# A SwiGLU FFN on one core in two parts of 6 and 5 column groups instead of three parts of 3, 4 and 4, with the residual h kept in DRAM in between

## The chip, the core and the metric

The kernel runs on one core of a Trainium2 chip. The metric is the device time of one execution in microseconds (us). The engines are TensorE (PE in the profile, with its weight loads as PEld), VectorE (DVE), ScalarE (ACT), GpSimd (POOL) and SyncE (SP). SP's instruction queue issues the weight loads and the DMA transposes, POOL's queue issues a few other DMAs. Engines and queues each work through their instructions in order and wait for one another by semaphores.

## The reference

Two pre-norm residual layers on a stream h of 256 tokens by 2048 columns, in float32. Layer 0 mixes with windowed attention and an mLSTM, layer 1 with forgetting attention. Each layer ends in the FFN that this study is about, and the last layer is followed by a norm:

```python
def swiglu(xn, w_gate, w_up, w_down):
    return (jax.nn.silu(xn @ w_gate) * (xn @ w_up)) @ w_down

h = h + mix
h = h + swiglu(rms_norm(h, norm_ffn[layer]), w_gate[layer], w_up[layer], w_down[layer])
```

w_gate and w_up are 2048 x 5632, w_down is 5632 x 2048.

## The kernel before

**Precision.** A float32 operand is split in two reduced parts, hi and lo (hi is a cast on ScalarE, lo the difference on VectorE: split_chunk, lines 184 to 191, for weights, split_plain, lines 355 to 357, for the rest). A product is three matmuls: hi x hi, hi x lo, lo x hi (three, lines 531 to 534). x is held as xh and xl, the FFN's middle result as mh and ml, each 16 blocks k of 128 rows by 256 tokens.

**Column groups.** pair_group (lines 539 to 635) computes two products of 512 columns at once (gate and up of the same columns, or two neighbouring column blocks of down), over the blocks k in pairs (256 rows of the weight). The constant ORDER, or DOWN for the down products, says in which order the pairs come and of which kind each is:

- A plain pair, (0, pair): 2 blocks x 2 token halves x 2 products x 3 = 24 matmuls of 512 columns. It loads 2 weight tiles of 512 KB and needs 2 pairs of hi/lo buffers.
- A mixed pair, (1, pair): the seven-product form of a 2 x 2 block product, 7 x 3 = 21 matmuls. It loads the same two tiles, and VectorE forms sums of weight blocks (lines 607 to 610), so that it needs 4 pairs of hi/lo buffers and sums of the left operand as well, made ahead by sums_of (lines 263 to 280) and kept in sx for x and sd for the middle result.

The products of the mixed pairs go to four PSUM banks (prod), the plain ones to four others (plain); from one group to the next the two sets of banks swap (par). Behind its last mixed pair a group combines prod into the tile c (combine, lines 553 to 565: a copy on ScalarE and three additions on VectorE). c has one buffer.

**Weight buffers.** In the FFN there are 8 pairs of hi/lo buffers in a ring (stock, lines 104 to 110 and 773) and 4 raw tiles for loads under way.

**The FFN** (lines 637 to 762). 5632 columns are 11 groups of 512, each a pair_group of gate and up with 8 pairs of which ORDER makes 3 mixed. After it VectorE adds the plain sums to c (line 665), ScalarE applies silu (line 667), VectorE multiplies (line 669). The result has tokens on the partitions and must be transposed to be the down product's left operand: as two 16-bit planes (copies at line 697), by DMA transposes on SP's queue (line 699), and then joined and split into mh and ml within the next group (join, lines 700 to 719, due at step MID or MID_DOWN, steps being positions of the order).

mh and ml hold 16 blocks, so 4 groups. PARTS = (0, 3, 7, 11) therefore makes three parts of 3, 4 and 4 groups; after each part two pair_groups (n0 = 0 and 2) multiply what is there by the matching rows of w_down, and VectorE adds the result to h: c at line 758, the plain sums in add_out (line 370). DOWN makes 2 of 6 pairs mixed in the first part and 3 of 8 in the others. In the first part, whose mh isn't full, the last group takes another way (lines 677 to 692): 8 transposes on TensorE (tile pf), split straight from PSUM. In the last part of layer 1 the second half of the columns is a plain gemm without mixed pairs (lines 743 to 748), and finish (lines 1292 to 1325) applies the final norm.

**Order of the instructions.** The program is written in the order above, and a scheduler places each engine's instructions ahead of time; run_due (lines 198 to 201) puts the due jobs behind a given cast. On the chip each engine keeps that order.

Of the kernel before, what the change touches and what calls it, by code (L numbers as in the profile page):

```python
# [17 lines left out]
P = 128  # L18
# [17 lines left out]
ORDER = ((0, 0), (1, 1), (0, 2), (1, 3), (0, 4), (1, 5), (0, 6), (0, 7))  # L36
HEAVY = ((1, 1), (0, 0), (1, 3), (0, 2), (1, 5), (0, 4), (1, 7), (0, 6))
FOURTH = 7
DENSE = ()
DOWN = {  # L40
    6: ((0, 0), (1, 1), (0, 2), (1, 3), (0, 4), (0, 5)),
    8: ((0, 0), (1, 1), (0, 2), (1, 3), (0, 4), (1, 5), (0, 6), (0, 7)),
}
MID = 6
MID_DOWN = 5
AHEAD = (5, 6)
# [29 lines left out]
def trunk(  # L76
# [278 lines left out]
    def split_plain(dst_h, dst_l, src):  # L355
        nc.scalar.copy(dst_h, src)  # L356
        nc.vector.tensor_tensor(out=dst_l, in0=src, in1=dst_h.bitcast(F32), op=ALU.subtract)  # L357
# [178 lines left out]
    def bank(par, name):  # L536
        return pm.tile([P, NB], F32, tag="pm", name=name) if par else pa.tile([P, NB], F32, tag="acc", name=name)
# [99 lines left out]
    def ffn(layer, fp, sx, x4, sd, key, todo, idx_next=None, key_next=None, finish=None):  # L637
        r = rstd(key)

        def sums_x(pair):  # L640
            if pair == FOURTH:
                return [[m[:, k, P:S] for k in (2, 6, 10)] + [x4[:, a, :]] for a, m in enumerate((xh, xl))]
            j = mixed_of(ORDER).index(pair)
            return four(sx[0], j), four(sx[1], j)

        for g0, g1 in zip(PARTS, PARTS[1:]):
            end = g1 == PARTS[-1]
            nk = 4 * (g1 - g0)
            order = DOWN[nk // 2]
            for g in range(g0, g1):  # L650
                par = (g1 - 1 - g) % 2
# [25 lines left out]
                if g == g1 - 1 and nk < 16:  # L677
                    for half in range(2):
                        pt = bank(par, "pf").rearrange("p (i q) -> p i q", i=2)
                        for i in range(2):  # L680
                            cs = (2 * half + i) * P
                            for t in range(NT):
                                nc.tensor.transpose(pt[:, i, t * P : (t + 1) * P], c[:, t, cs : cs + P], ident)
                        pair = 2 * (g - g0) + half
                        k = 2 * pair
                        split_plain(mh[:, k : k + 2, :], ml[:, k : k + 2, :], pt)
                        if pair in mixed_of(order):
                            j = mixed_of(order).index(pair)
                            sums_of(
                                fp, sd[0][:, j, :, :], sd[1][:, j, :, :], lambda full, pt=pt: nc.scalar.copy(full, pt)  # L690
                            )
                    continue
                cu = c.bitcast(U16).rearrange("p a (n b) -> p a n b", b=2)
                flat = c[:, 2:4, :].bitcast(U16).rearrange("p a n -> p (a n)").rearrange("p (b t n) -> p b t n", b=2, t=NT)
                turned = [fp.tile([P, 4, NT, P], U16, tag="tmp", name="turned") for _ in range(2)]
                for b in range(2):
                    nc.scalar.copy(flat[:, b, :, :], cu[:, 0:2, :, b])
                    for t in range(NT):
                        nc.sync.dma_start_transpose(turned[b][:, :, t, :], flat[:, b, t, :])
                def join(c=c, turned=turned, g=g, g0=g0, order=order):  # L700
# [4 lines left out]
                    k = 4 * (g - g0)  # L705
                    split_plain(
                        mh[:, k : k + 4, :].rearrange("p k s -> p (k s)"), ml[:, k : k + 4, :].rearrange("p k s -> p (k s)"), ct
                    )
                    for half in range(2):
                        pair = 2 * (g - g0) + half  # L710
                        if pair in mixed_of(order):
                            j = mixed_of(order).index(pair)
                            sums_of(
                                fp,
                                sd[0][:, j, :, :],
                                sd[1][:, j, :, :],
                                None,
                                ct[:, half * 512 : (half + 1) * 512].rearrange("p (i t q) -> p i t q", i=2, t=NT),
                            )

                todo = [(MID if g < g1 - 1 else MID_DOWN, join)]

            def sums_d(pair, order=order):
                j = mixed_of(order).index(pair)
                return four(sd[0], j), four(sd[1], j)

            def close(acc, n):
                if not end:
                    add_out(acc, n)
                elif idx_next is None:  # L730
                    finish(acc, n, gf)
                else:
                    add_out(acc, n)
                    if n < 1:
                        todo.append((LATER_DOWN[n], split_turned(idx_next, n, *scrap(fp, n))))
                    else:
                        split_scaled(idx_next, n)
                    square_sum(key_next, n)

            gf = None  # L740
            wd = w_down[layer][4 * g0 * P : 4 * g1 * P, :]
            for n0 in (0, 2):
                if end and idx_next is None and n0 == 2:
                    for n in (2, 3):
                        acc = new_acc()
                        gemm(acc, m_of, wd, n * NB, NB, 0, nk, nk, skew=3 if n == 3 else 1, halved=n == 3)
                        close(acc, n)
                    continue
                plain, c = pair_group(
                    fp, 1 - n0 // 2, m_of, sums_d, [(wd, n0 * NB), (wd, (n0 + 1) * NB)], order, todo  # L750
                )
                todo = []
                if end and idx_next is None:
                    gf = fp.tile([P, D], F32, tag="c", name="gf", bufs=1)
                    nc.gpsimd.dma_start(gf, norm_final.partition_broadcast(P))
                for t in range(NT):
                    o = h[:, t, n0 * NB : (n0 + 2) * NB]
                    nc.vector.tensor_tensor(
                        out=o, in0=c[:, 2 * t : 2 * t + 2, :].rearrange("p a n -> p (a n)"), in1=o, op=ALU.add
                    )  # L760
                for m in range(2):
                    close(plain[m], n0 + m)

    def close_layer(layer, w_out, idx, key, **rest):
        with tc.tile_pool(name=f"fp{layer}", bufs=2) as fp:
            nx = len(mixed_of(ORDER))
            nd = max(len(mixed_of(o)) for o in DOWN.values())
            sx = [fp.tile([P, nx, 4, P], F32R, name=f"sx{i}", bufs=1) for i in range(2)]
# [608 lines left out]
```

## Time and profile before

| | us |
|---|---|
| median of 3 runs | 2077.02 (2076.69 to 2077.94) |
| the profiled execution | 2077.56 |
| its span in the profile | 2075.9 |
| FFN of layer 0, first to last matmul | 322.4 to 1009.4 |
| FFN of layer 1, first to last matmul | 1379.6 to 2067.5 |

A table by stage gives each engine's busy time and, behind an x, its count of instructions in a stretch of the span, then the granted TensorE clock, the busy share of the 16 DMA engines, and GB/s. A row of a group of instructions has the line, the engine, the operation, output <- input, count, busy time and mean ns of one. A row of waits reads "who <- for whom: us in total, times, longest".

### The profile page before, as it was taken

How to read it: one execution, taken by the hardware profiler on the slowest of the kernel's cores; microseconds unless marked ns; L12 is line 12 of the kernel's file. 1: busy time of each engine (PE TensorE's matmuls, PEld its weight loads, DVE VectorE, ACT ScalarE, POOL GpSimd, SP SyncE). 2: the span in 40 equal slices, each digit the busy share in tenths (PEclk: the TensorE clock that was granted, in tenths of full speed). 3: DMA queues.
4: the chain of work that ended last, by engine and by line, in shares of the span. 5: the costliest groups of instructions: out<-in, count | busy, mean ns of one | idle time of the engine just before them, and what ended most of it. 6: DMA issues, size and time to landing. Idle time of an engine off the chain costs nothing.

```text
span 2075.9 us, 26965 instructions
## 1 busy us (share of the span) xinstructions
PE 2065.7 (100%) x9473; PEld 1715.1 (83%) x9473; DVE 1819.0 (88%) x2367; ACT 1373.7 (66%) x1744; POOL 44.6 (2%) x66
## 2 busy tenths in 40 slices
PE   9999999999999999999999999999999999999998
PEld 7878888888888888888888888888888888888886
DVE  6788769999999999999899688689999999999994
ACT  6777678664676656667676776687655666556763
POOL 1010000000000000000000001000000000000000
PEclk9999999999999999999999999999999999999999
DMA  8566577666677666766676776586756677667764
GB/s 292 169 216 192 188 244 238 206 219 196 210 223 224 193 208 217 222 204 183 206 213 209 231 201 183 155 268 217 233 187 218 209 217 224 202 195 225 206 196 141
DMA packets 309576, 434.88 MB, mean 209 GB/s; under 512 B 106412, under 2 KB 114624, under 8 KB 309312
## 3 DMA queue, kind: packets, MB, share of 16 engines
q1 hardware_dynamic: 307088, 426.27, 66.1%
q0 software_dynamic: 1632, 5.80, 0.8%
q8 instruction: 74, 1.21, 0.2%
q10 hardware_dynamic: 720, 1.09, 0.2%
q14 instruction: 62, 0.51, 0.1%
HBM read 408.68 MB, written 2.12 MB: 198 GB/s over the span
## 4 chain that ended last, share of the span: by engine, by line
PE 97%; DVE 1%; ACT 1%; issue 1%; DMA 0%; POOLq 0%; POOL 0%; ACTq 0%; DVEq 0%
PE acc L532 21%; PE acc L534 21%; PE acc L533 21%; PE acc L223 6%; PE acc L222 6%; PE acc L224 6%; PE prod L532 5%; PE prod L533 5%; PE prod L534 5%; PE p L386 1%; PE po L487 1%; ACT s L420 0%; PE po L488 0%; DVE lo L188 0%; DMA raw<-in_w_down_dram 0%
## 5 line engine op out<-in xcount | busy, mean ns | idle before, releaser
L188 DVE TENSOR_TENSOR lo<-raw,hi 128x1024 fp32r<-128x1024 f32 (+3 forms) x656 | 771.1, 1195 | 135.5 <-ACT hi L187 133.0
L187 ACT CAST hi<-raw 128x1024 fp32r<-128x1024 f32 (+3 forms) x656 | 661.7, 1027 | 341.2 <-PE acc L534 137.2
L533 PE MATMUL acc<-lo,xh 128*128 128x512 f32 x1320 | 514.0, 389 | 0.0
L534 PE MATMUL acc<-hi,xl 128*128 128x512 f32 x1320 | 511.4, 389 | 0.0
L532 PE MATMUL acc<-hi,xh 128*128 128x512 f32 x1320 | 506.2, 390 | 0.0
L534 PEld LDWEIGHTS acc<-hi,xl 128*128 128x128 f32 x1320 | 247.8, 188 | 51.6
L533 PEld LDWEIGHTS acc<-lo,xh 128*128 128x128 f32 x1320 | 247.8, 188 | 51.4 <-issue 0.2
L532 PEld LDWEIGHTS acc<-hi,xh 128*128 128x128 f32 x1320 | 247.7, 188 | 51.3 <-issue 0.2
L356 ACT CAST hi<-raw 128x512 fp32r<-128x512 f32 x204 | 166.9, 819 | 160.7 <-PE acc L534 83.6
L357 DVE TENSOR_TENSOR lo<-raw,hi 128x512 fp32r<-128x512 f32 x204 | 191.6, 939 | 11.4 <-ACT hi L356 10.4
L533 PE MATMUL acc<-lo,mh 128*128 128x512 f32 x466 | 181.0, 389 | 0.0
L534 PE MATMUL acc<-hi,ml 128*128 128x512 f32 x466 | 180.3, 389 | 0.0
L532 PE MATMUL acc<-hi,mh 128*128 128x512 f32 x466 | 176.2, 389 | 0.1
L356 ACT CAST hi<-t 128x1024 fp32r<-128x1024 f32 x95 | 100.0, 1053 | 63.9 <-PE acc L534 38.0
L357 DVE TENSOR_TENSOR lo<-t,hi 128x1024 fp32r<-128x1024 f32 x95 | 116.2, 1224 | 15.2 <-ACT hi L356 15.0
L223 PE MATMUL acc<-lo,mh 128*128 128x512 f32 (+1 forms) x322 | 126.3, 392 | 0.0
L222 PE MATMUL acc<-hi,mh 128*128 128x512 f32 (+1 forms) x322 | 125.8, 391 | 0.0
L224 PE MATMUL acc<-hi,ml 128*128 128x512 f32 (+1 forms) x322 | 123.7, 391 | 0.0
L532 PEld LDWEIGHTS acc<-hi,mh 128*128 128x128 f32 x466 | 87.5, 188 | 18.5 <-ACT hi L187 0.5
L534 PEld LDWEIGHTS acc<-hi,ml 128*128 128x128 f32 x466 | 87.5, 188 | 18.2
L533 PEld LDWEIGHTS acc<-lo,mh 128*128 128x128 f32 x466 | 87.4, 188 | 18.2
L223 PE MATMUL acc<-lo,xh 128*128 128x512 f32 (+3 forms) x288 | 100.0, 348 | 0.2 <-DVE lo L188 0.2
(356 smaller groups left out, 3174.7 us busy)
## 6 DMA issues: line engine op xcount, KB each, us to landing
raw<-in_w_gate_dram SPq DMA_DIRECT2D x176, 512.0 KB, 4.5
raw<-in_w_up_dram SPq DMA_DIRECT2D x176, 512.0 KB, 4.6
raw<-in_w_down_dram SPq DMA_DIRECT2D x176, 512.0 KB, 4.8
raw<-in_w_in_odd_dram SPq DMA_DIRECT2D x88, 512.0 KB, 5.3
raw<-in_w_in_even_dram SPq DMA_DIRECT2D x51, 512.0 KB, 5.1
raw<-in_w_out_even_dram SPq DMA_DIRECT2D x32, 512.0 KB, 5.2
raw<-in_w_out_odd_dram SPq DMA_DIRECT2D x32, 512.0 KB, 4.7
hr<-in_w_in_even_dram SPq DMA_DIRECT2D x12, 512.0 KB, 4.5
```

Of the source, the lines that this page charges most:

```text
L187: latest[0] = nc.scalar.copy(hi[:, k, 0:n], raw[:, k, 0:n])
L188: nc.vector.tensor_tensor(out=lo[:, k, 0:n], in0=raw[:, k, 0:n], in1=hi[:, k, 0:n].bitcast(F32), op=ALU.subtract)
L222: nc.tensor.matmul(o, ah[:, ts], hi, start=(k == 0), stop=False)
L223: nc.tensor.matmul(o, ah[:, ts], lo, start=False, stop=False)
L224: nc.tensor.matmul(o, al[:, ts], hi, start=False, stop=(k == k_all - 1 and cs.stop == n))
L356: nc.scalar.copy(dst_h, src)
L357: nc.vector.tensor_tensor(out=dst_l, in0=src, in1=dst_h.bitcast(F32), op=ALU.subtract)
L386: nc.tensor.matmul(pq[j % 2][:, j // 2, :], q_of(j, b), k_of(j)[:, 0:cols], start=True, stop=True)
L487: nc.tensor.matmul(po, v_of(j, 0), tt[:, j, 0:2, :].rearrange("p c q -> p (c q)"), start=True, stop=False)
L532: nc.tensor.matmul(o, ah, hi, start=start, stop=False)
L533: nc.tensor.matmul(o, ah, lo, start=False, stop=False)
L534: nc.tensor.matmul(o, al, hi, start=False, stop=stop)
```

## The change

PARTS becomes (0, 6, 11): 6 groups, a down product of 12 pairs, 5 groups, a down product of 10 pairs. Room for the extra blocks of the middle result comes from h. At the start of the FFN h is stored to DRAM (kept) on POOL's queue, in two halves, and the buffer of h takes the blocks from 16 on (the tile more). The first part's down result isn't added to h by VectorE: VectorE adds the plain sums to c, and an accumulating DMA on POOL's queue adds c to kept. At the start of the second part h is loaded back. In the second part the blocks from 16 on (over) are in the buffers of sx, which are free by then. 4 pairs of each down product are mixed: 1, 3, 5, 7 of 12 and 1, 3, 5, 8 of 10; the sums of the fourth have no room in sd and lie in an unused part of mh and ml, or in over. All groups now take the way of the DMA transposes; the branch with transposes on TensorE is gone. Line numbers of the changed kernel differ.

```diff
+NK2 = 8
 DOWN = {
-    6: ((0, 0), (1, 1), (0, 2), (1, 3), (0, 4), (0, 5)),
-    8: ((0, 0), (1, 1), (0, 2), (1, 3), (0, 4), (1, 5), (0, 6), (0, 7)),
+    12: tuple((int(pair in (1, 3, 5, 7)), pair) for pair in range(12)),
+    10: tuple((int(pair in (1, 3, 5, 8)), pair) for pair in range(10)),
 }
+DOWN_FOURTH = {12: 7, 10: 8}
-PARTS = (0, 3, 7, 11)
+PARTS = (0, 6, 11)
...
+        kept = dp.tile([P, NT, D], F32, name=f"kept{layer}")
+        for cs in (slice(0, D // 2), slice(D // 2, D)):
+            nc.gpsimd.dma_start(kept[:, :, cs], h[:, :, cs])
...
         for g0, g1 in zip(PARTS, PARTS[1:]):
...
+            if end:
+                h = cp.tile([P, NT, D], F32, tag="h", name="h")
+                for cs in (slice(0, D // 2), slice(D // 2, D)):
+                    nc.gpsimd.dma_start(h[:, :, cs], kept[:, :, cs])
+            else:
+                more = cp.tile([P, 2, NK2, S], F32R, tag="h", name="more")
+                over = more[:, 0, :, :], more[:, 1, :, :]
+            def room_of(pair, order=order, fourth=fourth, end=end):
+                if pair != fourth:
+                    j = mixed_of(order).index(pair)
+                    return sd[0][:, j, :, :], sd[1][:, j, :, :]
+                if end:
+                    return tuple(m[:, 4:6, :].rearrange("p a (b q) -> p (a b) q", b=2) for m in over)
+                return mh[:, 2:15:4, P:S], ml[:, 2:15:4, P:S]
...
-                if g == g1 - 1 and nk < 16:
-                    for half in range(2):
-                        pt = bank(par, "pf").rearrange("p (i q) -> p i q", i=2)
-                        for i in range(2):
-                            cs = (2 * half + i) * P
-                            for t in range(NT):
-                                nc.tensor.transpose(pt[:, i, t * P : (t + 1) * P], c[:, t, cs : cs + P], ident)
...
-                    continue
...
+            if end:
+                over = [fp.tile([P, 6, S], F32R, tag=f"sx{i}", name=f"over{i}", bufs=1) for i in range(2)]
...
+                if not end:
+                    for m in range(2):
+                        for t in range(NT):
+                            o = c[:, 2 * t + m, :]
+                            nc.vector.tensor_tensor(out=o, in0=plain[m][t], in1=o, op=ALU.add)
+                    nc.gpsimd.dma_start(
+                        kept[:, :, n0 * NB : (n0 + 2) * NB],
+                        c.rearrange("p (t m) n -> p t (m n)", t=NT),
+                        accum_op=ALU.add,
+                    )
+                    continue
```

More of the change, by code (lines that the diff above doesn't have):

```diff
@@ L644, in sums_x, with mid, mid_of @@
             return four(sx[0], j), four(sx[1], j)
+        nonlocal h
+        par = 1
+        kept = dp.tile([P, NT, D], F32, name=f"kept{layer}")
+        for cs in (slice(0, D // 2), slice(D // 2, D)):
+            nc.gpsimd.dma_start(kept[:, :, cs], h[:, :, cs])
+        over = None
+        def mid(k, n):
+            if k < KT:
+                return mh[:, k : k + n, :], ml[:, k : k + n, :]
+            return tuple(m[:, k - KT : k - KT + n, :] for m in over)
+        def mid_of(k):
+            return tuple(m[:, 0, :] for m in mid(k, 1))
         for g0, g1 in zip(PARTS, PARTS[1:]):
@@ L649, in ffn @@
             order = DOWN[nk // 2]
+            fourth = DOWN_FOURTH[nk // 2]
+            if end:
[12 more added lines that the diff above has]
+                return mh[:, 2:15:4, P:S], ml[:, 2:15:4, P:S]
             for g in range(g0, g1):
-                par = (g1 - 1 - g) % 2
+                par = 1 - par
                 plain, c = pair_group(
@@ L676, in ffn @@
                     )
-                if g == g1 - 1 and nk < 16:
-                    for half in range(2):
-                        pt = bank(par, "pf").rearrange("p (i q) -> p i q", i=2)
-                        for i in range(2):
-                            cs = (2 * half + i) * P
-                            for t in range(NT):
[L683 to L691, printed above, removed]
-                    continue
                 cu = c.bitcast(U16).rearrange("p a (n b) -> p a n b", b=2)
@@ L699, in ffn, with join @@
                         nc.sync.dma_start_transpose(turned[b][:, :, t, :], flat[:, b, t, :])
-                def join(c=c, turned=turned, g=g, g0=g0, order=order):
+                def join(c=c, turned=turned, k=4 * (g - g0), order=order, room_of=room_of):
                     ct = c[:, 0:2, :].rearrange("p a n -> p (a n)")
@@ L704, in join @@
                         nc.scalar.copy(cb[:, :, b], turned[b].rearrange("p k t q -> p (k t q)"))
[L705 to L708, printed above, removed]
+                    split_plain(*(m.rearrange("p k s -> p (k s)") for m in mid(k, 4)), ct)
                     for half in range(2):
-                        pair = 2 * (g - g0) + half
+                        pair = k // 2 + half
                         if pair in mixed_of(order):
-                            j = mixed_of(order).index(pair)
                             sums_of(
                                 fp,
-                                sd[0][:, j, :, :],
-                                sd[1][:, j, :, :],
+                                *room_of(pair),
                                 None,
@@ L721, in ffn, with sums_d @@
                 todo = [(MID if g < g1 - 1 else MID_DOWN, join)]
-            def sums_d(pair, order=order):
-                j = mixed_of(order).index(pair)
-                return four(sd[0], j), four(sd[1], j)
+            if end:
+                over = [fp.tile([P, 6, S], F32R, tag=f"sx{i}", name=f"over{i}", bufs=1) for i in range(2)]
+            def sums_d(pair, room_of=room_of):
+                return [[m[:, e, :] for e in range(4)] for m in room_of(pair)]
             def close(acc, n):
-                if not end:
-                    add_out(acc, n)
-                elif idx_next is None:
+                if idx_next is None:
                     finish(acc, n, gf)
-                else:
[L733 to L738, printed above, removed]
+                    return
+                add_out(acc, n)
+                if n < 1:
+                    todo.append((LATER_DOWN[n], split_turned(idx_next, n, *scrap(fp, n))))
+                else:
+                    split_scaled(idx_next, n)
+                square_sum(key_next, n)
             gf = None
@@ L745, in ffn @@
                         acc = new_acc()
-                        gemm(acc, m_of, wd, n * NB, NB, 0, nk, nk, skew=3 if n == 3 else 1, halved=n == 3)
+                        gemm(acc, mid_of, wd, n * NB, NB, 0, nk, nk, skew=3 if n == 3 else 1, halved=n == 3)
                         close(acc, n)
                     continue
+                par = 1 - par
                 plain, c = pair_group(
-                    fp, 1 - n0 // 2, m_of, sums_d, [(wd, n0 * NB), (wd, (n0 + 1) * NB)], order, todo
+                    fp, par, mid_of, sums_d, [(wd, n0 * NB), (wd, (n0 + 1) * NB)], order, todo
                 )
                 todo = []
-                if end and idx_next is None:
+                if not end:
[9 more added lines that the diff above has]
+                    continue
+                if idx_next is None:
                     gf = fp.tile([P, D], F32, tag="c", name="gf", bufs=1)
@@ L766, in close_layer @@
             nx = len(mixed_of(ORDER))
-            nd = max(len(mixed_of(o)) for o in DOWN.values())
-            sx = [fp.tile([P, nx, 4, P], F32R, name=f"sx{i}", bufs=1) for i in range(2)]
+            nd = 3
+            sx = [fp.tile([P, nx, 4, P], F32R, tag=f"sx{i}", name=f"sx{i}", bufs=1) for i in range(2)]
             x4 = fp.tile([P, 2, P], F32R, name="x4", bufs=1)
```

## The prediction

> **What bounds the kernel now.** I read the page first: the busy shares and the chain of work that ended last.
>
> ```profile
> span 2075.9 us, 26965 instructions
> ...
> PE 2065.7 (100%) x9473; PEld 1715.1 (83%) x9473; DVE 1819.0 (88%) x2367; ACT 1373.7 (66%) x1744; POOL 44.6 (2%) x66
> ...
> PE 97%; DVE 1%; ACT 1%; issue 1%; DMA 0%; POOLq 0%; POOL 0%; ACTq 0%; DVEq 0%
> ```
>
> TensorE is idle for 2075.9 - 2065.7 = 10.2 us of the whole span, and the chain runs through it for 97%. VectorE at 88% is a possible second bound. A busy TensorE can still be a slow one, so the next view is the table by stage: five stretches of the FFN, cut where one kind of matmul ends and the next begins, and the last gemm.
>
> ```profile
> core 0: us, PE busy (x) PEld busy (x) DVE busy (x) ACT busy (x) POOL busy (x), PEclk, DMA share, GB/s
> 446.84:510.96 64.12, 64.01 (x286) 52.69 (x285) 60.91 (x71) 34.44 (x39) 0.00 (x0) 1.00 0.63 199
> 676.65:759.61 82.96, 82.96 (x367) 68.69 (x366) 75.82 (x86) 48.31 (x51) 0.00 (x0) 1.00 0.66 209
> 759.61:925.53 165.92, 165.92 (x733) 137.39 (x732) 157.58 (x193) 107.45 (x117) 0.00 (x0) 1.00 0.69 213
> ...
> 1504.05:1567.76 63.71, 63.71 (x286) 52.77 (x285) 60.91 (x71) 34.21 (x39) 0.00 (x0) 1.00 0.63 200
> ...
> 1982.33:2023.81 41.48, 41.48 (x184) 34.35 (x183) 37.55 (x41) 28.92 (x31) 0.00 (x0) 1.00 0.57 179
> 2023.81:2067.51 43.70, 43.70 (x199) 36.29 (x197) 22.81 (x32) 15.47 (x25) 1.15 (x2) 1.00 0.36 122
> ```
>
> The third row is four gate/up groups. By the code each has 3 mixed pairs of 21 matmuls and 5 plain pairs of 24, so 183, and 4 x 183 = 732 (the row counts one more, across the edge). 165.92 / 732 = **0.2267 us** per matmul of 512 columns. The down product of a four-group part (second row) is 2 x 183 = 366 in 82.96 us: 0.2267 again. So while VectorE is 91 to 95% busy (75.82 / 82.96, 157.58 / 165.92), TensorE never waits: the FFN is paced by the number of matmuls. Only the down product of the first, three-group part (first and fourth rows) is longer than its count: 2 x (2 x 21 + 4 x 24) = 276 matmuls are 62.57 us, and the rows have 64.12 and 63.71. The excess is **1.55 us** in layer 0 and **1.14 us** in layer 1. Its contents are the TensorE transposes and, in layer 0, one wait:
>
> ```profile
> L683 PE MATMUL pf<-ident,c x16: 270/272/273, 460.7 to 1520.9; 128*128 128x128 f32 x16
> ```
> ```profile
> 462.57 5.61 DMA raw<-in_w_down_dram
> ...
> 469.16 1.05 ACT hi L187
> 470.21 0.04 issue
> 470.26 0.50 PE acc L532
> ```
>
> The chain of waits there comes from a weight load through ScalarE's cast to a matmul at 470.26. It's the only place inside an FFN where the chain leaves TensorE for long: 1.55 - 1.14 = 0.41 us.
>
> **The change part by part.**
>
> *Matmuls.* Mixed pairs of the down products, each saving 3 matmuls: before, layer 0 has 2 x (2 + 3 + 3) = 16, layer 1 has 2 x 2 + 2 x 3 + 3 = 13 (its last half is a plain gemm). After, layer 0 has 2 x (4 + 4) = 16, layer 1 2 x 4 + 4 = 12. One is lost: 3 x 0.2267 = **+0.68 us**. All other matmuls stay.
>
> *Transposes.* The branch with the 16 TensorE transposes goes; with it go the excess of both rows and the wait at 470: -1.55 - 1.14 = **-2.69 us**. The wait could come back elsewhere (a rival below). In their place the last group of part one is turned by DMA, as all others are: two ScalarE copies out, four DMA transposes on SP's queue, two copies back, a split. SP's queue waits for the copies with weight loads behind it, 20 times already:
>
> ```profile
> SPq L699 <- ACT c L697: 45.2, 20, 4.4
> ACT hi L187 <- PE acc L534: 137.4, 94, 4.6
> ACT hi L356 <- PE acc L534: 121.9, 93, 3.0
> ```
>
> ```profile
> turned<-c SPq DMA_TRANSPOSE x80, 2.5
> ```
>
> SP's wait (45.2 us in 20) is 2.3 us each time, and the stretches that hold those groups run at 0.2267 us per matmul, so two more cost nothing. The cover is in the two ScalarE rows: it waits 94 + 93 = 187 times for TensorE to give a weight buffer back, so it is normally as far ahead as the 8 buffers allow. A mixed pair takes 4, a plain one 2; with the pair in use subtracted that is about one plain pair, 24 x 0.2267 = 5.4 us, ahead (an estimate). Without that cover each would cost up to its 2.3 us. The rows that feed the last pairs must be joined at step 5; they're wanted at pair 8 (second part) or 10 (first), against pair 6 before: later, so free.
>
> *VectorE.* A down pair group now costs it a combine and six additions into h:
>
> ```profile
> L370 DVE TENSOR_TENSOR h<-acc,h 128x512 f32<-128x512 f32 x56 | 36.3, 691 | 3.5 <-PE acc L224 3.5
> L758 DVE TENSOR_TENSOR h<-c,h 128x1024 f32<-128x1024 f32 x22 | 26.0, 1225 | 0.0
> L559 DVE TENSOR_TENSOR c<-prod,c 128x1024 f32<-128x1024 f32 x33 | 40.4, 1223 | 0.0
> L558 DVE TENSOR_TENSOR c<-prod,c 128x512 f32<-128x512 f32 x33 | 22.7, 688 | 0.0
> ```
>
> Combine 2 x 0.69 + 1.22 = 2.60, adding c 2 x 1.23 = 2.45, adding the plain sums 4 x 0.69 = 2.76: 7.81 us. Per layer two whole groups go (15.6) and two more lose the 2.45: -20.5 us, 41 in all, some 2% of 1819. On the path it is worth nothing, since no FFN row shows TensorE waiting for VectorE; a negative bound of zero follows from the 0.2267 in rows where VectorE is 95% busy.
>
> *DMAs.* Per layer POOL's queue stores h (2 x 1 MB), adds two 1 MB tiles to it in DRAM, and loads it back (2 x 1 MB). The trace has no accumulating DMA and no store of this size. The nearest rows are a 1 MB load on POOL's queue, weight loads beside it, and the 11 us from 221 to 232 in which POOL's queue loads 2.1 MB of x:
>
> ```profile
> raw<-in_w_down_dram SPq DMA_DIRECT2D x3, 512.0 KB, 7.2
> gf<-in_norm_final_dram POOLq DMA_DIRECT2D x1, 1024.0 KB, 8.1
> ```
> ```profile
> q0 software_dynamic: 576, 2.10, 49.4%
> q1 hardware_dynamic: 917, 1.77, 46.3%
> ```
> ```profile
> 221.00:232.00 11.00, 11.00 (x59) 9.37 (x58) 8.26 (x13) 5.87 (x7) 2.90 (x4) 1.00 0.96 351
> ```
>
> Both bursts cost TensorE no idle time: 11.00 of 11.00 us here, 43.70 of 43.70 us in the last gemm beside the 8.1 us load. I cost the plain transfers at 0. An accumulate reads two and writes one: bounds 8.1 us (as the load) and 3 x 8.1 x 2 = 48.6 us (three passes, at half the DMA engines as above). I take 2 x 8.1 = 16.2, nearest to the load's row. The Trainium skill, "DMA: Bandwidth & Descriptors", section "Anatomy of one DMA", fits 2.0 us + bytes / 436e3 for a plain DMA of this kind. By it, an estimate, 1 MB takes 4.4 us where the row has 8.1, and three passes 9.2; the sum would be the same.
>
> *The new waits.* (a) c has one buffer, so the next combine's ScalarE copy waits for the accumulate to finish reading; the casts of the next weights are queued behind it. At the same place in layer 0 now:
>
> ```profile
> L370 DVE TENSOR_TENSOR h<-acc,h x4: 692/693/694, 761.4 to 764.4; 128x512 f32<-128x512 f32 x4
> ```
> ```profile
> L555 ACT COPY c<-prod x1: 580/580/580, 786.6 to 786.6; 128x512 f32<-128x512 f32 x1
> ```
>
> ```profile
> L755 POOL DMA_DIRECT2D gf<-in_norm_final_dram x1: 580/580/580, 2024.9 to 2024.9; - x1
> ```
>
> The last addition ends at 765.1 and the copy starts at 786.6: 21.5 us, less 0.6 for issuing the DMA (gf's row), so 20.9 us of room against 16.2. (b) Reloading h waits for the accumulates and for the last reader of the tile that took h's place, but h is wanted only after five gate/up groups, 5 x 183 x 0.2267 = 207 us; nothing but those DMAs and the next norm's small work queues behind on POOL. (c) The tile in h's place is first written after four groups, 166 us. All free.
>
> *Sum.* -2.69 + 0.68 = **-2.0 us**. The profiled execution took 2077.56 us (span 2075.9 and 1.7 around it), 0.5 above the median of 2077.02; so 2075.5 for it, and **2075.0** beside the median.
>
> **The rivals.**
>
> *A, slower: weight loads wait behind POOL's bursts.* In the burst above SP's queue got 46.3% of the DMA engines; the FFN rows need 0.66. In 11 us it falls (0.66 - 0.463) x 11 / 0.66 = 3.3 us behind. The change makes four such bursts per layer (store, two accumulates at 2 MB of reading each, reload), eight in all. Uncovered: 26 us, to 2101. It decides where less than 3.3 us of weights is ready: when ScalarE isn't waiting for TensorE, right after a part change. If a third of them hit it, 8.8 us: 2083.8. Against it: both bursts above cost nothing, and 5.4 us is ahead on average. For it: 470.26 shows the cover can run out, and there a weight load was late. The Trainium skill, same page, section "Issuing engines are not separate DMA queues", says that DMAs of all issuers run on the same 16 engines and interleave; the 49.4 and 46.3% agree.
>
> *B, slower: the accumulate holds c.* It decides at 20.9 + 5.4 = 26 us to landing. At 40 us it costs 13.7 us once per layer (the first accumulate has 8 pairs, some 40 us, of room): 27 us, 2102; at the upper bound 45 us.
>
> *C: PSUM banks come free too late.* The second part's last mixed pair is pair 8 of 10, so one plain pair follows, not two, and the next group's plain sums take the banks of prod. Now, in the group that ends at 2023.81, on TensorE and then VectorE:
>
> ```profile
> 2012.03 0.39 PE L534 MATMUL prod<-hi,sd 128*128 128x512 f32 x1
> ```
> ```profile
> 2019.63 1.22 DVE L559 TENSOR_TENSOR c<-prod,c 128x1024 f32<-128x1024 f32 x1
> ```
>
> The last bank is free 2020.85 - 2012.25 = 8.6 us after the last product. After the change the next group starts 27 matmuls, 6.1 us, after it, wants its second bank at 6.8 and its fourth at 9.5. Given out in order of release that's no stall; in the order of their names the bank freed last is the second wanted, 1.8 us at three places: 2080.4. If VectorE is later still, more.
>
> *D, faster by over 4 us:* VectorE's relief would have to shorten TensorE's path, but there is nothing in the FFN beyond the 2.69 us to win. Only a better instruction order elsewhere could give it.
>
> *E, nothing happens:* the transposes are hidden already. Against it: they sit in TensorE's own queue, and the excess is in both rows.
>
> **How the numbers follow.** The likeliest is the sum, with E and stalls under 4 us beside it. A difference under 0.2%, 4.2 us, is about what a measurement here can tell from none. Forecast within +-1.5 us 0.58; E 0.02; C 0.12, a third of it past 4.2 us; A 0.14, B 0.09; D 0.05. Faster by over 0.2%: 0.05. Slower: 0.04 + 0.14 + 0.09 = 0.27. Within: 0.68. The range goes from 2073.0 (the forecast less 2) to 2086.0, which takes in C, E and A at a third; it leaves out D, B and A's upper part, under 0.2.
>
> **What would show it.** No pf rows; transposes turned from c up from 80 to 88; the two down products of the first part at 552 x 0.2267 = 125.1 us, those of layer 0's second at 456 x 0.2267 = 103.4 and its own later transposes; VectorE's busy time down by 41 us; TensorE's idle time in the FFN near zero. A is right if matmuls of the FFN wait for casts that wait for raw; B if ScalarE's copy at line 555 waits for a DMA; C if matmuls into acc wait for VectorE's combine. I'm wrong if TensorE's idle time grows by over 4 us.

## The result and the profile after

| | before, us | after, us |
|---|---|---|
| median of 7 runs | 2077.80 (2076.69 to 2079.83) | 2084.53 (2083.77 to 2085.69) |
| the profiled execution | 2077.56 | 2084.70 |
| its span | 2075.9 | 2083.0 |

The ratio is 1.0033, with a 95% interval of 1.0021 to 1.0045. The change made the kernel 6.7 us slower. The prediction had 2075.0, with 0.68 on no difference and 0.27 on slower: the direction was missed, though the time lies in the range.

The first lines of the page of the changed kernel:

```profile
span 2083.0 us, 26898 instructions
...
PE 2066.7 (99%) x9460; PEld 1713.5 (82%) x9460; DVE 1784.4 (86%) x2315; ACT 1380.4 (66%) x1744; POOL 53.5 (3%) x78
```

VectorE is 34.6 us less busy and TensorE has 13 matmuls and transposes fewer, yet the span is 7.1 us longer. TensorE is idle for 2083.0 - 2066.7 = 16.3 us of it, against 10.2. The table by stage shows where, cut at TensorE's first matmul of each stage, with the columns of the prediction. Three stages: the whole first part of layer 0 (its gate/up groups and its down product), layer 0's second down product, and the first part of layer 1:

```profile
322.77:698.23 375.46, 374.38 (x1651) 309.69 (x1651) 345.01 (x421) 251.29 (x283) 2.55 (x3) 1.00 0.72 221
905.63:1013.04 107.41, 105.01 (x465) 86.05 (x464) 95.32 (x117) 66.99 (x85) 0.00 (x0) 1.00 0.59 183
1382.85:1760.97 378.12, 375.50 (x1651) 309.31 (x1650) 344.56 (x421) 251.13 (x283) 2.56 (x3) 1.00 0.71 219
```

The same view in another cut, with the first part's down product in layer 0, the second part's five gate/up groups there, and the last down product of layer 1:

```profile
573.11:698.23 125.12, 125.12 (x554) 103.60 (x552) 108.65 (x122) 71.26 (x74) 1.16 (x1) 1.00 0.72 224
698.23:905.63 207.40, 207.40 (x917) 171.73 (x915) 191.82 (x231) 135.54 (x148) 2.62 (x3) 1.00 0.73 226
...
1968.37:2074.50 106.13, 106.13 (x475) 88.10 (x473) 73.73 (x88) 53.54 (x66) 1.13 (x2) 1.00 0.50 159
```

These three have no idle time and give the pace: 552 matmuls in 125.12 us and 915 in 207.40 are 0.2267 us each, as before. The first three rows are too long for their counts.

- **The first part** (first and third row): 6 x 183 + 552 = 1650 matmuls are 374.06 us. Layer 0 has 1.4 us more, and its first matmul came 322.77 - 322.40 = 0.4 us late; layer 1 has 4.1 more. Together **5.9 us**, none of it in the down products, which are at the pace in both layers (125.12 us each).
- **The end of layer 0's FFN** (second row): 107.41 us. 456 matmuls are 103.38, and before, the same stage had 83.86 us for 366 matmuls (82.97), so 0.89 of transposes and edges:

```profile
925.53:1009.39 83.86, 83.86 (x375) 69.48 (x374) 76.19 (x93) 56.19 (x73) 0.00 (x0) 1.00 0.59 172
```

That leaves **3.1 us** of the 107.41.

With the two terms that were forecast this makes -2.69 + 0.68 + 5.9 + 3.1 = 7.0 us, and the spans differ by 7.1.

**What the first stall waits for.** The waits from 1380 to 1425 of the changed kernel, and TensorE's own view of the longest stall there:

```profile
ACT box L324 <- DMA box<-box: 3.1, 1, 3.1
...
ACT hi L189 <- DMA raw<-in_w_up_dram: 2.1, 1, 2.1
...
ACT hi L189 <- DMA raw<-in_w_gate_dram: 1.8, 1, 1.8
```
```profile
1415.84 0.50 PE L534 MATMUL prod<-hi,sx 128*128 128x512 f32 x1 [1.40 <-ACT hi L358]
```

TensorE waits for casts of weights. But the casts don't wait longer for their loads: at the same place before, the two rows of raw are 1.9 and 1.7 us. What is new is the first row. Box is h itself, which is turned by DMA transposes for the first group's left operand; ScalarE copies it back at line 324, and the casts of the first group's weights are queued behind that copy. SP's queue issues eight transposes there, four at a time, and the copy waits for the fourth. This one with who waited for it, then the store beside it, then the fourth transpose at the same place before:

```profile
L319 SPq DMA_TRANSPOSE box<-box x1: 1267/1267/1267, 1388.7 to 1388.7; - x1
...
who waited for it (us, times):
  ACT box L324: 3.1, 1
...
DMA to landing us min/median/max: 6.1/6.1/6.1
```
```profile
1388.81 0.68 POOL L652 DMA_DIRECT2D kept<-h  x1 [46.38 <-DVE h L372]
```
```profile
L317 SPq DMA_TRANSPOSE box<-box x1: 1266/1266/1266, 1383.1 to 1383.1; - x1
...
DMA to landing us min/median/max: 2.5/2.5/2.5
```

The transpose was issued 0.1 us ahead of the second half of the store, and landed after 6.1 us instead of 2.5. SP's queue also issues more slowly there (the two weight loads behind the transpose take 1.30 and 1.16 us to issue, not 0.53 and 0.41), but they come after it, and the copy doesn't wait for them. What the two queues moved (q0 is POOL's, q1 SP's; packets, MB, share of the 16 DMA engines), in 1.5 us of the store (1391 to 1392.5), and while the same transpose ran in the kernel before (1384 to 1385.3):

```profile
q0 software_dynamic: 134, 0.55, 92.1%
q1 hardware_dynamic: 132, 0.03, 9.9%
```
```profile
q1 hardware_dynamic: 544, 0.13, 49.8%
```

The transpose consists of some 500 packets of 0.25 KB. Alone they took 1.3 us. Beside the store they went one for one with packets of 4 KB, 132 against 134, and so got 9.9% of the engines.

In layer 0 the first half of the store is the one that hits: it starts at 281.0 us, 0.1 us behind the second of eight transposes, which land after up to 6.6 us (before: up to 3.1). ScalarE's copy waits 1.2 us, and at the start of the FFN its copies of h come 2.4 us later than before, while TensorE's first matmul comes 0.4 us later. All in all ScalarE waits 5.2 us for transposes of h, in three places; in the kernel before it never does.

Of all 36 transposes of h, the medians and maxima from issue to landing are these, after and then before:

```profile
DMA to landing us min/median/max: 2.4/3.2/7.3
```
```profile
DMA to landing us min/median/max: 2.4/2.5/5.2
```

**What the second stall waits for.** VectorE at the end of layer 0's FFN, after and then before:

```profile
1008.73 1.22 DVE L561 TENSOR_TENSOR c<-prod,c 128x1024 f32<-128x1024 f32 x1
1009.98 2.36 DVE L783 TENSOR_TENSOR h<-c,h 128x1024 f32<-128x1024 f32 x2
1012.26 1.28 DVE L372 TENSOR_TENSOR h<-acc,h 128x512 f32<-128x512 f32 x2
```
```profile
1001.09 1.22 DVE L559 TENSOR_TENSOR c<-prod,c 128x1024 f32<-128x1024 f32 x1
...
1004.00 2.35 DVE L758 TENSOR_TENSOR h<-c,h 128x1024 f32<-128x1024 f32 x2
```

The combine ends at 1009.95, which is 3.1 us before TensorE goes on with the next stage (1013.04). Before, it ended at 1002.31, which is 7.1 us before that point (1009.4, the end of the FFN). The additions into h come after it, and TensorE's next work is a transpose of h for layer 1:

```profile
1011.43 0.39 PE L536 MATMUL acc<-hi,over 128*128 128x512 f32 x1
1013.04 0.41 PE L291 MATMUL pt<-ident,h 128*128 128x128 f32 x2 [1.22 <-issue]
```

For the other half of the columns the same additions lie some 50 us earlier. The chain of waits there runs through them and box to a matmul that starts late, at 977.86:

```profile
959.84 2.27 DVE h L783 x2
...
964.38 1.81 DVE h L372 x3
...
974.20 2.47 ACT box L324 x2
```
```profile
977.86 0.47 PE L534 MATMUL prod<-hi,sd 128*128 128x512 f32 x1 [1.09 <-DVE xl L364]
```

### The profile page after: what moved, and what is told of

It reads as the page before. It is cut to its first block, busy times and chain, and to the rows that moved or that the text cites. A ratio compares the mean times of both kernels' runs of the same rounds, so it can differ in the third digit from the quotient of the medians.

```text
span 2083.0 us, 26898 instructions
## 1 busy us (share of the span) xinstructions
PE 2066.7 (99%) x9460; PEld 1713.5 (82%) x9460; DVE 1784.4 (86%) x2315; ACT 1380.4 (66%) x1744; POOL 53.5 (3%) x78
## 4 chain that ended last, share of the span: by engine, by line
PE 89%; ACT 4%; DMA 2%; DVE 2%; issue 2%; SPq 0%; POOLq 0%; POOL 0%; ACTq 0%; DVEq 0%
PE acc L536 20%; PE acc L535 20%; PE acc L534 20%; PE prod L536 5%; PE prod L534 5%; PE prod L535 5%; PE acc L225 4%; PE acc L224 4%; PE acc L226 4%; ACT hi L189 1%; ACT box L324 1%; DMA box<-box 1%; PE p L388 1%; DVE lo L190 1%; ACT xh L363 1%
## 5 line engine op out<-in xcount | busy, mean ns | idle before, releaser
L225 PE MATMUL acc<-lo,mh 128*128 128x512 f32 x320 | 125.9, 394 | 0.0
L224 PE MATMUL acc<-hi,mh 128*128 128x512 f32 x320 | 125.4, 392 | 0.0
L226 PE MATMUL acc<-hi,ml 128*128 128x512 f32 x320 | 123.3, 392 | 0.0
L536 PE MATMUL acc<-hi,ml 128*128 128x512 f32 x302 | 117.6, 389 | 0.0
L535 PE MATMUL acc<-lo,mh 128*128 128x512 f32 x302 | 117.5, 389 | 0.0
L534 PE MATMUL acc<-hi,mh 128*128 128x512 f32 x302 | 115.7, 389 | 0.0
L226 PE MATMUL acc<-hi,xl 128*128 128x512 f32 (+3 forms) x288 | 98.8, 344 | 0.0
L224 PE MATMUL acc<-hi,xh 128*128 128x512 f32 (+3 forms) x288 | 96.1, 347 | 0.3
L534 PE MATMUL prod<-hi,sx 128*128 128x512 f32 x198 | 77.4, 391 | 2.5 <-ACT hi L358 2.5
```

Of the source, the lines that this page charges most:

```text
L224: nc.tensor.matmul(o, ah[:, ts], hi, start=(k == 0), stop=False)
L225: nc.tensor.matmul(o, ah[:, ts], lo, start=False, stop=False)
L226: nc.tensor.matmul(o, al[:, ts], hi, start=False, stop=(k == k_all - 1 and cs.stop == n))
L534: nc.tensor.matmul(o, ah, hi, start=start, stop=False)
L535: nc.tensor.matmul(o, ah, lo, start=False, stop=False)
L536: nc.tensor.matmul(o, al, hi, start=False, stop=stop)
```

## The experiments

**Theory 1:** the store of h costs the 5.9 us, since SP's transposes of h fall into it. **Theory 2:** the late last mixed pair (8 of 10) costs the 3.1 us, since h's last additions hang on its combine. The main rival of both was the prediction's A: weight loads wait behind any of the bursts, accumulates and reloads too. (In the expectations "Theory 1" is each time the theory that the experiment tests.)

### The store a group later (e1_late_store, e1b_late_store_fill)

```diff
-        for cs in (slice(0, D // 2), slice(D // 2, D)):
-            nc.gpsimd.dma_start(kept[:, :, cs], h[:, :, cs])
+        def store():   # called behind the pair_group of g == 1; more is allocated there too
+            mark = nc.gpsimd.tensor_copy(MARK, mh[:, 0, 0:1].bitcast(F32))
+            with tc.issue_after(mark.ins):
+                for cs in (slice(0, D // 2), slice(D // 2, D)):
+                    nc.gpsimd.dma_start(kept[:, :, cs], hs[:, :, cs])
```

In e1 MARK is a new tile of 4 bytes per partition, in e1b a spare column of fill.

> The changed kernel with one thing undone: the two stores of h to DRAM start only once the first group's middle result has been joined (some 75 us into the FFN), not at its start. Theory 1 (the 4 KB packets of the store hold back the DMA transposes at the FFN's start, and ScalarE, which waits for them, delays the first group): the stalls of TensorE in the first group go, 1.7 us in layer 0 and 4.0 us in layer 1, so 5.7 us faster than the changed kernel, about 2078.8 us. Rival 2 (the store takes DMA time from the weight loads, wherever it stands): the stalls move with it, about 2084.5 us. Rival 3 (the order that the scheduler chose is at fault, not the store): no change, 2084.5 us.

2100.49 us, ratio 1.0108 (1.0094 to 1.0121): none of the outcomes that were named. The stalls of the first groups were gone, but all matmuls of the FFN were 0.230 us apart: the first part took 379.66 us, without idle time, for the same 1650 matmuls that are 374.06 at 0.2267. The new tile was the suspect, and the next version avoids it.

> The late store again, but its marker writes into a tile that exists already, so that no address in SBUF moves: the first try had a new 4-byte tile, and all its matmuls of the FFN were 0.230 us apart, not 0.2267. Theory 1 (the store holds back the DMA transposes at the FFN's start): the stalls of the first groups go and the matmuls are 0.2267 us apart: about 2078.8 us, of which 3.1 us are still stalls at the end of layer 0's FFN. Rival 4 (it wasn't the 4 bytes; the late store itself slows the matmuls): about 2100 us again.

2079.25 us (2078.16 to 2080.87), ratio 1.0006 (0.9997 to 1.0015), 5.3 below the changed kernel (the kernel before had 2078.20 beside it and 2077.80 beside the changed one, so some tenths of a us of such a difference can belong to the series of runs). The three stages of e1b (first part of layer 0, layer 0's second down product, first part of layer 1):

```profile
322.30:696.30 374.00, 374.00 (x1652) 309.69 (x1651) 342.00 (x417) 248.79 (x279) 3.56 (x5) 1.00 0.72 224
903.70:1011.21 107.51, 105.05 (x466) 86.06 (x464) 96.14 (x119) 68.22 (x87) 0.00 (x0) 1.00 0.59 182
1381.58:1755.75 374.17, 374.17 (x1651) 309.61 (x1650) 342.74 (x418) 249.31 (x280) 3.53 (x5) 1.00 0.71 224
```

The store now falls among plain weight loads, the first parts run at the pace (374.06), and the second row keeps its 3.1 us. Both halves are issued back to back there and land after 9.4 to 14.0 us, later than in the changed kernel (5.3 to 6.5), and cost nothing. So it isn't the burst alone that costs, but the burst beside the transposes.

### The last mixed pair earlier (e2_pair7, e2b_pair7_layer0)

```diff
-    10: tuple((int(pair in (1, 3, 5, 8)), pair) for pair in range(10)),
+    10: tuple((int(pair in (1, 3, 5, 7)), pair) for pair in range(10)),
-DOWN_FOURTH = {12: 7, 10: 8}
+DOWN_FOURTH = {12: 7, 10: 7}
```

In e2 layer 1's last gemm reads the sums of the fourth pair in place of four quarter blocks of mh and ml (so too in e3_both below). e2b has the new order in layer 0's second part alone, and computes everything.

> The changed kernel with the second part's mixed pairs at 1, 3, 5, 7 instead of 1, 3, 5, 8, so that two plain pairs follow the last mixed one; the sums of the fourth lie in the unused part of mh and ml as in the first part. Same count of matmuls. Theory 1 (the late mixed pair delays the combine, so h of layer 0 is complete only after its group has ended and TensorE waits with the last transposes): the 3.1 us of stalls between 976 and 1013 us go, about 2081.4 us. Rival 3 (they come from something else at the layer's end, as the reloaded h or the order): no change, 2084.5 us.

2080.75 us, ratio 1.0013 (1.0004 to 1.0022), as expected.

> The changed kernel with the mixed pairs 1, 3, 5, 7 in the second part of layer 0 only, where the stalls stood; layer 1 as in the changed kernel. Theory 1 (late combine): as with the first try, about 2080.8 us, the stalls between 976 and 1013 us gone and those of the first groups still there. Rival (the first try was faster through layer 1, whose order it changed too): about 2084.5 us.

2081.43 us (2077.65 to 2082.35), ratio 1.0011 (1.0003 to 1.0020), 3.1 below the changed kernel. The second and third of the three stages in e2b:

```profile
906.40:1010.70 104.30, 104.30 (x465) 86.32 (x464) 94.11 (x113) 67.59 (x87) 0.00 (x0) 1.00 0.61 183
1380.46:1755.35 374.89, 374.34 (x1652) 309.61 (x1650) 344.69 (x420) 251.25 (x281) 2.56 (x3) 1.00 0.70 221
```

The first row is at 104.30: 103.38 for the matmuls and 0.92 for the rest, as before the change (0.89). One plain pair, 24 x 0.2267 = 5.4 us, was enough for the whole 3.1. This row, and not the median, is the measure: the eleven runs fall in two groups, around 2079 and 2082, and the profiled one (2079.01) is of the lower. In the second row the store still costs, 0.8 us here and not 4.1. In this execution its second half started 1.0 us behind the fourth transpose, which landed after 2.6 us; in the changed kernel it was 0.1 us, and 6.1.

### Both (e3_both, e3b_both_fill)

> Both edits, the late store and the mixed pairs at 1, 3, 5, 7. If theory 1 names all that the change added, what is left is the sum of the prediction, the transposes gone and three more matmuls, 2.0 us below the kernel before: about 2075.8 us. If either cause is another, it stays above 2078 us.

2097.40 us, ratio 1.0094 (1.0080 to 1.0108): it has the new tile of e1, and its slow matmuls.

> Both: late store with the marker in an existing tile, and the mixed pairs 1, 3, 5, 7 in the second part of layer 0. If the two causes are all that the change added, 2.0 us below the kernel before: about 2075.9 us, and no gap of more than 0.5 us between matmuls in either FFN. If a third cause is left, above 2077.9 us.

2075.91 us (2075.43 to 2076.78), ratio 0.9990 (0.9981 to 0.9999): faster than both kernels, by 2.3 us against before and 8.6 against the changed one.

```profile
322.94:697.28 374.34, 374.33 (x1651) 309.61 (x1650) 342.88 (x418) 249.31 (x280) 5.58 (x5) 1.00 0.71 224
904.68:1008.98 104.30, 104.30 (x465) 86.32 (x464) 94.21 (x113) 67.65 (x87) 0.00 (x0) 1.00 0.60 183
1378.71:1753.08 374.37, 374.29 (x1651) 309.61 (x1650) 342.05 (x417) 248.45 (x277) 3.53 (x5) 1.00 0.71 223
```

With both causes taken away, what is left is the sum of the prediction: -2.3 measured (the interval reaches from -0.2 to -3.9), -2.0 forecast. The rows show no idle time of more than 0.1 us.

### The store alone, in the kernel before (e4_before_store, e5_store_512B)

```diff
         r = rstd(key)
+        kept = dp.tile([P, NT, D], F32, name=f"kept{layer}")
+        for cs in (slice(0, D // 2), slice(D // 2, D)):
+            nc.gpsimd.dma_start(kept[:, :, cs], h[:, :, cs])
```

> The kernel before with the two stores of h to DRAM added at the start of each FFN and nothing reading them. Theory 1: the store alone brings the stalls of the first group, 1.7 and 4.0 us: 5.7 us above the kernel before, about 2083.5 us. Rival 3 (the order or another part of the change): the store alone costs nothing, 2077.8 us.

2080.21 us (2078.66 to 2086.53), ratio 1.0013 (1.0004 to 1.0022). The stall appears in a kernel that has nothing else of the change, at the same matmul. The first three groups of each layer in e4, and its first stall:

```profile
322.64:448.52 125.88, 124.87 (x550) 103.04 (x550) 119.96 (x160) 96.04 (x118) 1.40 (x2) 1.00 0.73 231
1382.26:1508.04 125.78, 124.84 (x549) 103.08 (x550) 119.88 (x160) 95.92 (x118) 1.41 (x2) 1.00 0.73 231
```
```profile
352.96 0.50 PE L532 MATMUL prod<-hi,sx 128*128 128x512 f32 x1 [1.01 <-ACT hi L356]
```

Before, each of these stages took 124.44 us. The size was missed: 2.3 us where 5.7 was expected, and single runs of this kernel differ by 7.9 us. In the profiled one the second half of the store started 0.5 us (layer 0) and 0.4 us (layer 1) behind the fourth transpose, which landed after 3.1 and 3.3 us. Beside the 0.1 us and 6.1 of the changed kernel, and the 1.0 us and 2.6 of e2b, this makes the price a matter of some tenths of a us. That it is so in the runs without a profile too isn't shown.

e5 writes the same bytes as rows of 512 bytes in DRAM, by four DMAs.

> The kernel before with the same stores of h as e4, the same bytes, but into rows of 512 bytes, so eight times as many packets of an eighth of the size. Theory 1 (a DMA engine takes turns by packets, so a transpose's small packet waits for a 4 KB one each time): the transposes get through beside the store, and less than half of the extra 2.3 us of e4 is left: below 2079.0 us. Rival 2 (the store's bytes take the DMA time): as e4, 2080.2 us or more.

2080.63 us, ratio 1.0014 (1.0005 to 1.0023), nothing gained. It doesn't tell the theories of the cause apart, since the packets did not become smaller: POOL's queue moved its 1.05 MB in 288 packets in e5 and in 272 in e4.

### Any burst (e7_dram_to_dram)

```diff
+            mark = nc.gpsimd.tensor_copy(fill[:, 12:13], h[:, 0, cs.stop - 1 : cs.stop])
+            with tc.issue_after(mark.ins):
+                nc.gpsimd.dma_start(kept[:, :, cs], xv[:, :, cs])
```

This is e4 with copies from DRAM to DRAM, so that the transfers on POOL's queue read neither h nor anything else in SBUF.

> The kernel before with two 1 MB copies from DRAM to DRAM on POOL's queue at the places of e4's stores (a one-element copy on POOL waits for the same halves of h). If any burst on POOL's queue holds back SP's transposes there: as e4, 2.3 to 2.9 us above the kernel before, about 2080.7. If it is the store's reading of SBUF: no change, 2078.2.

2086.44 us (2084.75 to 2087.69), ratio 1.0041 (1.0028 to 1.0053). The landing of the transposes in e7, and the first three groups of layer 0, which take 124.44 us before:

```profile
DMA to landing us min/median/max: 2.4/4.6/9.5
```
```profile
323.56:451.32 127.76, 125.49 (x550) 102.88 (x550) 120.08 (x160) 96.18 (x118) 1.55 (x3) 1.00 0.71 226
```

So reading h isn't the cause. The price was missed, 8.3 us where 2.3 to 2.9 were expected. At least two things differ from e4, and the run doesn't part them: each copy landed after 6.5 to 9.1 us (e4's stores after 5.3 to 6.3), and the second half started earlier, about 0.1 us ahead of the third transpose, so that in both layers the third and the fourth landed after 5.7 to 7.7 us.

### The transposes alone (e6_turned_alone)

```diff
-                if g == g1 - 1 and nk < 16:
+                if False:
-                todo = [(MID if g < g1 - 1 else MID_DOWN, join)]
+                todo = [(MID if g < g1 - 1 else MID_DOWN if nk > 12 else 3, join)]
```

The kernel before, with its three parts, but the last group of the first part turned by DMA.

> The kernel before, three parts, with only the TensorE transposes replaced: the last group of the first part is turned by DMA as the others are, and joined at step 3 of the down product's 6 pairs. Prediction's term: the 2.69 us of the two rows go, about 2075.5 us beside 2078.2. Rival: three pairs, some 16 us, aren't enough for copies, DMA transposes, copies back and split, TensorE waits in both layers, and it's slower than the kernel before; the longer order of 12 pairs is then what makes the exchange possible.

2090.95 us (2089.92 to 2092.72), ratio 1.0064 (1.0051 to 1.0076). TensorE in e6 behind the place where the joined rows are wanted:

```profile
472.27 0.80 PE L532 MATMUL acc<-hi,mh 128*128 128x512 f32 x1 [4.88 <-ACT mh L356]
472.86 0.63 PE L533 MATMUL acc<-lo,mh 128*128 128x512 f32 x1
473.28 0.63 PE L532 MATMUL acc<-hi,mh 128*128 128x512 f32 x1
```

With 6 pairs, joined at step 3, the rows are late by 4.9 us, and by 4.2 in layer 1. The exchange of the transposes isn't free by itself; it is in the order of 12 pairs that PARTS = (0, 6, 11) brings, where the first part's down product has no idle time (125.12 of 125.12 us). An earlier join in the 6 pairs wasn't tried.

### Shifted tiles (e8_shift_4B, e9_shift_64B)

```diff
+    pad = sm.tile([P, 1], F32, tag="pad", name="pad", bufs=1)
+    nc.gpsimd.memset(pad, 0.0)
```

The kernel before with an unused tile of 4 bytes per partition in pool sm (e8), or of 64 bytes (e9, [P, 16]). Nothing else differs.

> The kernel before with one unused tile of 4 bytes per partition ahead of the layers' tiles, nothing else. If the shift of addresses explains the first late store (0.230 us between matmuls, 22 us in all), matmuls are again slower than 0.2267 us and the time is some 15 to 25 us above the kernel before. If not: 2078.2.

2098.60 us, ratio 1.0099 (1.0085 to 1.0113). The down product whose 366 matmuls took 82.96 us, in e8:

```profile
681.57:765.56 83.99, 83.99 (x368) 68.69 (x366) 77.07 (x87) 48.50 (x51) 0.00 (x0) 1.00 0.66 207
```

> The same with 64 bytes per partition. If only the alignment counts, not the extra tile: as the kernel before, 2078.2 us. Otherwise as e8.

2094.80 us, ratio 1.0081 (1.0066 to 1.0097), the same stage in 83.87 us. A tile that nothing uses is enough for slow matmuls as in e1 and e3, and a multiple of 64 bytes doesn't mend it.

## Why the prediction was right and wrong

**Right: the sum.** The first part's down product took 125.12 us (forecast 125.1) and the eight more transposes of c by DMA (88 instead of 80) that replace TensorE's cost nothing there. e3b, where only the sum is left, came out 2.3 us below before.

**Right: VectorE's relief is worth nothing.** It is 34.6 us less busy (41 forecast), and every stage without a stall has the old pace.

**Right, but its size by luck: the accumulate (wait a), rival B.** It costs nothing. It lands after 10.4 to 16.3 us, where 16.2 was taken against 20.9 of room:

```profile
L772 POOL DMA_DIRECT2D kept<-c x4: 1110/1152/1168, 637.1 to 1762.5; - x4
...
DMA to landing us min/median/max: 10.4/13.6/16.3
```

ScalarE's copy into c waited for no DMA, and the stages beside the accumulates and the reload have no idle time. But 16.2 was twice a load's 8.1, for the second reading, and the four landings point to another reason. The first accumulate of each layer had POOL's queue to itself and landed after 10.4 and 11.2 us (a reload alone on it: 8.9 and 8.8); the second, with 16.0 and 16.3, was issued 0.7 us behind a reload. The Trainium skill, "DMA: Bandwidth & Descriptors", section "Anatomy of one DMA", would give, as an estimate by its fit, 4.4 us for a store of 1 MB and 9.2 for three passes. The stores landed after 5.3 to 6.5 us and the accumulates after up to 16.3; the measurement decides.

**Wrong: "I cost the plain transfers at 0".** This is the step that failed first, by 5.3 us in the medians (e1b) and 5.9 in the rows. The two bursts in which it was grounded ran beside weight loads, for which ScalarE has buffers in stock; so does the moved store of e1b, and it is free too. In the changed kernel the store runs where SP's queue issues the transposes of h, and for these there is no stock: they are on the path from the last addition into h to the first matmuls of the FFN. The prediction asked what the bytes cost, not which DMAs are in flight beside them. Its 46.3% for SP's queue held for loads, whose packets are of some 2 KB (1.77 MB in 917); a transpose with packets of 0.25 KB got 9.9%.

Rival A had a place ("right after a part change"), and at a third its 8.8 us are not far from the 5.9. That is luck, for it had the wrong victim and the wrong bursts: the waits for raw did not grow, and of the store, the accumulates and the reload only the store cost anything.

**Wrong: the late last mixed pair weighed by PSUM banks alone.** Rival C saw that the combine would be late, and asked only who wants its banks; what hangs on h was put at nothing, without a reason. No bank was late: layer 1's last down products, with the same order in the first of them, have no idle time (106.13 of 106.13 us). What was late is h: in layer 0 the next layer waits for the additions behind the combine, 3.1 us (e2b). In layer 1 the final norm follows, and TensorE has nothing to do after it.

**Open.** Packets taken in turn explain that the transpose's data came slowly, not all of its lateness: in the 1.5 us above, 132 packets went where alone some 500 took 1.3 us, but it landed only at 1394.8 us, 0.2 us behind the store. What held back its end wasn't found. The same page of the Trainium skill, section "Queues, rings and completion order", has each DMA engine take turns between queues by the packet: the counts of 132 and 134 agree, though a packet of that page holds several descriptors, and no run here shows that it is what the profile counts. e5 was meant to test the turns and did not change the packets.

## What to carry to other kernels

Before a transfer is called hidden, look up which DMAs are in flight beside it and who waits for those: weight loads with buffers in stock forgave bursts of 1 and 2 MB here, DMA transposes on the path did not forgive 1 MB, and moved away from them the same store was free. When an instruction moves to a later place in a group, follow all that hangs on its result into the next stage, not only the buffers that it holds. And read a surprise by its pace first: a new tile of 4 bytes cost more than all the rest.

## What the runs showed of the hardware

- **DMA transposes beside a burst.** A transpose of 0.13 MB, in packets of 0.25 KB, landed after 6.1 us instead of 2.5 when a store of 1 MB in packets of 4 KB started 0.1 us behind it. The two queues' packets went one for one (132 and 134 in 1.5 us).
- **An unused tile changed the matmul's pace.** 4 bytes per partition raised the time between matmuls from 0.2267 to 0.2295 us (82.96 and 83.99 us for 366) and the kernel's time by 20.4 us; 64 bytes did so by 16.6. The granted clock was 1.00 in these rows. What such a tile changes, as far as is known, is where later tiles lie; which property of the addresses decides wasn't found.
- **Matmuls after an idle time.** In e6, after 4.9 us without work, matmuls came 0.43 us apart (472.86, 473.28, 473.71), not 0.23, and the granted clock was 0.50 from 472.27 to 475. In layer 1, after 4.2 us, the first ones came 0.24 us apart, and only from 1 us after the restart the clock was 0.50 (1537 to 1540), with TensorE busy. The Trainium skill, "TensorE: Matmul & The Clock Gate", section "Part 1: The HAM clock gate", has the clock halved after an idle window of some 3.4 us and gives 426.7 ns for 512 columns then: the trace agrees.
- **An accumulating DMA** of 1 MB into DRAM landed after 10.4 and 11.2 us beside weight loads, with nothing else on its queue; a plain load of that size from DRAM after 8.8 and 8.9.
